# A fast down product's sum goes to the residual through ScalarE and an accumulating DMA

## The chip, the cores and the metric

The kernel runs on one core of a Trainium2 chip. A core has a matrix engine (TensorE, PE in the profile; its weight loads are the row PEld), three engines for elementwise work (VectorE, DVE; ScalarE, ACT; GpSimd, POOL), an engine that only issues DMAs here (SyncE, SP), and 16 DMA engines that all queues share. Engines run their own instruction streams in order and wait for each other on semaphores. Matmuls write to PSUM, a small memory that VectorE and ScalarE read; all else lies in SBUF.

The metric is device time in microseconds, lower is better: 2209.68 us before the change, the median of three runs (2209.25 to 2211.64).

## The reference

A two-layer encoder over 528 tokens (512 and 16 learned ones) of width 1024. A layer is FFN, mixer, FFN; the change touches the FFNs alone.

```python
def swiglu(x, w_gate, w_up, w_down):
    return (jax.nn.silu(x @ w_gate) * (x @ w_up)) @ w_down
...
    for l in range(DEPTH):
        h = h + 0.5 * swiglu(rmsnorm(h, norm_gains[l, 0]),
                             ffn_w_gate[l, 0], ffn_w_up[l, 0], ffn_w_down[l, 0])
        h = h + mixer(rmsnorm(h, norm_gains[l, 1]), ...)
        h = h + 0.5 * swiglu(rmsnorm(h, norm_gains[l, 2]),
                             ffn_w_gate[l, 1], ffn_w_up[l, 1], ffn_w_down[l, 1])
    return rmsnorm(h, final_norm)[:, N_META:]
```

All of it is float32. Width of the hidden layer: 2816, that is 22 chunks of 128, handled as 11 pairs.

## The kernel before

**Numbers.** Activations lie with channels on the 128 partitions and tokens along the row, in chunks of 128 channels; `hall` holds the residual `h`, eight chunks of 528 tokens. TensorE multiplies in a format with fewer bits, so each operand is split into a high part (`hi`, a rounding cast by ScalarE) and a low part (`lo`, the difference, by VectorE), and each product is three matmuls: hi by hi, hi by lo, lo by hi. Weights are split in the same way: ScalarE casts a block of 128 x 1024 (`whi`, L287), VectorE subtracts (`wlo`, L288). `W.make` runs that three to four blocks ahead of TensorE, `W.fetch` loads nine ahead on SP's queue.

**Seven products for eight.** The FFN's products are done by a fast scheme on 2 x 2 blocks (the block rows of the weights, and two halves of the tokens or the channels), with seven products named 1 to 7 where the plain way has eight. The sums of weight blocks that it needs are made partly by VectorE (L253, L256, L297) and partly by accumulating DMAs on GpSimd's queue (`W.add`, L208), each behind a plain load of the other summand. One product is 24 matmuls.

**The down projection.** The 11 pairs of hidden chunks are handled in groups of 4, 4 and 3 (`GROUPS`). The first two groups' down products use the seven-product scheme (`fast_down`, steps "S"): for each of two halves of the output chunks (`dq` 0 and 1), seven products accumulate in PSUM. Products 1, 6, 7 and 4 share one accumulator ("X"), 2 has its own ("Y"), 5 and 3 share one ("Z"). After each product the accumulator's running sum, 128 x 2 x 264 (for the last FFN 128 x 2 x 256), is added to two residual chunks' half (L719, L720), while accumulation goes on for the next product on top of it. So the next product on the same accumulator waits until the sum has been read. The third group is done in the plain way (`down`).

A block of such products, one for each of two groups in each of four FFNs, so eight blocks, is written out in `ffn_steps`: parts of products 1, 2 and 5 for `dq` 0 (three of the four hidden pairs, before the last pair is ready), then their rest, and then eleven products in the order that `AB` gives, `dq` in turn: 1 of dq 1, 6, 2 of dq 1, 7, 3, 4, and 6, 5, 7, 3, 4 of dq 1. Between the last five stand the first products of the next pair of the up projection (1, 2, 6, 5; L598).

The operands of the down products ("1", "2", "5", "6", "7", "3", "4") are made from the block's hidden values: differences by VectorE (`difference`, L678), the high part by ScalarE (L673, L670), the low part by VectorE (L674, L671). Operand "6" is made last of those that the block's start needs.

**What sets the order.** The tile framework's scheduler orders each engine's instructions within what the program's dependencies allow; pools of buffers set the waits. Touched pools: `t` (six tiles of 128 x 528), `wsa` and `wsb` (three each, sums of weights), `wraw` (three plain weight blocks), `whi` and `wlo` (four each), and the PSUM pairs (four). GpSimd's queue carries the weight sums' accumulating DMAs and nothing else. The residual is read again by the next block's adds, by the third group's adds (L564) and, after those, by the next norm.

Of the kernel before, what the change touches and what calls it, by code (L numbers as in the profile page):

```python
# [14 lines left out]
ALU = mybir.AluOpType  # L15
# [313 lines left out]
def build(tc, ctx, xt, wts, win, par, w2, const, umask, out):  # L329
    nc = tc.nc  # L330
    V, S, G, TE = nc.vector, nc.scalar, nc.gpsimd, nc.tensor
# [30 lines left out]
    def nm(p):  # L362
        count[0] += 1
        return f"{p}{count[0]}"
# [3 lines left out]
    def slot(tag, dtype=F32, n=None):  # L368
        return slots[tag].tile([P, T], dtype, tag=tag, name=nm(tag))[:, : n or live[0]]
# [11 lines left out]
    def pair(second=False):  # L381
        return (slots["s2"] if second else pss).tile([P, 2, 512], F32, tag="s2" if second else "ss", name=nm("ss"))
# [27 lines left out]
    def v2(ap):  # L410
        return ap.rearrange("p (a b) -> p a b", a=2)
# [161 lines left out]
    def ffn(l, f, norm, done, following):  # L573
# [112 lines left out]
        def operands_behind(g, dq, c):  # L686
            if (dq, c) == (1, "1"):
                difference(g, 1, 1, 3)
                operand(g, "7")
            elif (dq, c) == (1, "2"):  # L690
                operand(g, "3")
                difference(g, 2, 2, 0)
                operand(g, "4")

        def fast_down(g, dq, c, part):
            last = sum(GROUPS[: g + 1]) - 1
            kinds = ("ss", "s2") if last % 2 == 0 else ("s2", "ss")
            st = made.setdefault(("S", g, dq), {})
            where = {"2": "Y", "5": "Z", "3": "Z"}.get(c, "X")
            begin = c in "125"  # L700
            if part != 2:
                if begin:
                    st[where] = pair(kinds[{"Y": 0, "Z": 1, "X": dq}[where]] == "s2")
                st["w"] = st.get("w", {})
                st["w"][c] = W.op((l, f), NPAIR + QUADS * g + dq, c, ahead=AHEAD_MADE - 1)
            acc = st[where][:, :, :w]
            hi, lo = st["w"][c]
            xs = sets[g, c]
            for k in {1: range(3), 2: range(3, 4), 3: range(4)}[part]:
                for j in range(2):  # L710
                    for i, (a, b) in enumerate(((hi, 0), (hi, 1), (lo, 0))):
                        TE.matmul(acc[:, j], a[:, j, k], xs[b][:, k], start=bool(begin and k == 0 and i == 0),  # L712
                                  stop=k == 3 and i == 2, skip_group_check=not begin)
            if part == 1:
                return
            st["w"].pop(c)
            for m, q in {"1": [(0, 0)], "2": [(0, 0)], "5": [(1, 1)], "6": [(0, 1)], "3": [(0, 1)], "7": [(1, 1)],
                         "4": [(1, 0)]}[c]:
                to = hall[:, 4 * dq + m : 4 * dq + m + 3 : 2, q * w : (q + 1) * w]  # L719
                V.tensor_tensor(to, to, acc, ALU.add)  # L720
            if dq == 1:
                sets.pop((g, c))
            operands_behind(g, dq, c)
# [24 lines left out]
        for i, step in enumerate(steps):  # L748
            if step[0] == "P":
                if step[1:] == (0, "5") and norm.acc is None:  # L750
                    for c in range(KC):
                        norm.square(c)
                product_of_pair(*step[1:])
                if step[1:] == (0, "5"):
                    rs, up = norm.rs(True)
                    W.behind = prev_act[0]
                if step[1] in (2, 3) and step[2] in "6574":
                    m = next(risen)
                    V.scalar_tensor_tensor(h(m), h(m), -1.0, up, ALU.mult, ALU.mult)
                if i == last_op:  # L760
                    close_pools(norm.pools)
                    following()
            elif step[0] == "S":
                fast_down(*step[1:])
            elif step[0] == "O":
                g, last = step[1:]
                ks = slice(3, 4) if last else slice(0, 3)
                operands_of(g, ks, "215" if last else "125")
                difference(g, 0, 3, 0, ks)
                if last:  # L770
                    operand(g, "6")
            else:
                down(*step[1:])
# [597 lines left out]
```

## Time and profile before

| what | value |
|---|---|
| runs | 2209.68 us median, 2209.25 to 2211.64, n = 3 |
| profiled execution, its own time | 2211.05 us |
| its span, first to last instruction | 2209.2 us |
| granted TensorE clock | 0.997 |
| HBM read | 289.94 MB |

The profile is of one execution. Its page gives the busy time and share of each engine, the DMA queues, the chain of work that ended last (followed back from the last instruction, each step to what released it or to the instruction before it on its engine), and groups of instructions by source line. A row of instructions reads: line, engine, operation, destination tile <- source tiles, shapes. In a timeline a row begins with start and duration in us, and the bracket at its end is idle time of that engine before it and who ended it. In a table of waits a row is "who <- for whom: us in total, times, longest". In a table of windows a row is the stretch, its length, busy us and (instructions) of PE, PEld, DVE, ACT and POOL, the granted clock, the mean share of the 16 DMA engines that is busy, and GB/s. Matmuls are pipelined, so their durations overlap and add up to more than the time they take.

### The profile page before, as it was taken

How to read it: one execution, taken by the hardware profiler on the slowest of the kernel's cores; microseconds unless marked ns; L12 is line 12 of the kernel's file. 1: busy time of each engine (PE TensorE's matmuls, PEld its weight loads, DVE VectorE, ACT ScalarE, POOL GpSimd, SP SyncE). 2: the span in 40 equal slices, each digit the busy share in tenths (PEclk: the TensorE clock that was granted, in tenths of full speed). 3: DMA queues.
4: the chain of work that ended last, by engine and by line, in shares of the span. 5: the costliest groups of instructions: out<-in, count | busy, mean ns of one | idle time of the engine just before them, and what ended most of it. 6: DMA issues, size and time to landing. Idle time of an engine off the chain costs nothing.

```text
span 2209.2 us, 40079 instructions
## 1 busy us (share of the span) xinstructions
PE 2162.4 (98%) x16506; PEld 2070.2 (94%) x16506; DVE 1785.4 (81%) x2703; ACT 1214.1 (55%) x1779; POOL 101.8 (5%) x120
## 2 busy tenths in 40 slices
PE   7999999999999999999999999999999999999998
PEld 6999999989999999999999999999788888999997
DVE  7897978486886689889789979775879767997987
ACT  7544545344785555454575445453457836554543
POOL 1000000000000001000010000000000001000100
PEclk9999999999999999999999999999999999999999
DMA  9775753212113468666567757432121145776752
GB/s 268 189 204 160 191 152 106 82 49 68 49 39 122 114 167 205 190 182 187 162 163 186 207 164 191 143 110 77 49 84 51 42 133 152 198 202 181 189 165 67
DMA packets 87463, 311.41 MB, mean 141 GB/s; under 512 B 9712, under 2 KB 12144, under 8 KB 87280
## 3 DMA queue, kind: packets, MB, share of 16 engines
q1 hardware_dynamic: 68624, 245.53, 32.9%
q0 software_dynamic: 16704, 60.82, 15.8%
q8 instruction: 130, 2.13, 0.4%
q10 hardware_dynamic: 1952, 2.50, 0.4%
q14 instruction: 53, 0.43, 0.1%
HBM read 289.94 MB, written 2.10 MB: 132 GB/s over the span
## 4 chain that ended last, share of the span: by engine, by line
PE 81%; DVE 11%; ACT 4%; issue 2%; DMA 2%; SPq 0%; DVEq 0%; ACTq 0%
PE ss L598 37%; PE mm L465 13%; PE ss L712 11%; PE ss L465 10%; PE sm L465 2%; DVE wlo L288 2%; DMA w<-win 2%; PE sm L1074 1%; PE ss L1049 1%; DVE g L678 1%; ACT whi L287 1%; PE sm L1090 1%; DVE h L720 1%; PE ss L471 1%; PE sm L1091 1%
## 5 line engine op out<-in xcount | busy, mean ns | idle before, releaser
L598 PE MATMUL ss<-xc,whi 128*128 128x264 f32 (+1 forms) x4928 | 907.2, 285 | 15.5 <-ACT whi L287 7.4
L598 PEld LDWEIGHTS ss<-xc,whi 128*128 128x128 f32 x4928 | 767.2, 189 | 20.4 <-ACT c L602 8.4
L598 PE MATMUL ss<-xc,wlo 128*128 128x264 f32 (+1 forms) x2464 | 702.5, 285 | 8.8 <-DVE wlo L288 8.8
L598 PEld LDWEIGHTS ss<-xc,wlo 128*128 128x128 f32 x2464 | 466.5, 189 | 11.1 <-DVE wlo L288 10.9
L288 DVE TENSOR_TENSOR wlo<-w,whi 128x1024 fp32r<-128x1024 f32 (+1 forms) x337 | 408.1, 1217 | 63.4 <-ACT whi L287 63.2
L287 ACT CAST whi<-w 128x1024 fp32r<-128x1024 f32 (+1 forms) x337 | 350.0, 1050 | 163.3 <-PE ss L598 80.5
L465 PE MATMUL mm<-x,whi 128*128 128x264 f32 (+1 forms) x1712 | 384.6, 315 | 0.0
L465 PEld LDWEIGHTS mm<-x,whi 128*128 128x128 f32 x1712 | 278.3, 188 | 16.5 <-issue 1.0
L465 PE MATMUL mm<-x,wlo 128*128 128x264 f32 (+1 forms) x856 | 266.0, 315 | 0.0
L712 PE MATMUL ss<-g,whi 128*128 128x264 f32 (+1 forms) x1280 | 237.4, 284 | 0.0
L287 ACT CAST whi<-raw 128x1024 fp32r<-128x1024 f32 x126 | 132.3, 1050 | 163.4 <-PE mm L465 102.3
L602 ACT COPY c<-ss 128x528 f32<-128x528 f32 (+1 forms) x132 | 78.5, 594 | 258.6 <-PE ss L598 258.6
L288 DVE TENSOR_TENSOR wlo<-raw,whi 128x1024 fp32r<-128x1024 f32 x126 | 153.9, 1222 | 59.0 <-ACT whi L287 58.1
L712 PEld LDWEIGHTS ss<-g,whi 128*128 128x128 f32 x1280 | 198.4, 188 | 0.1
L712 PE MATMUL ss<-g,wlo 128*128 128x264 f32 (+1 forms) x640 | 181.3, 283 | 0.0
L465 PEld LDWEIGHTS mm<-x,wlo 128*128 128x128 f32 x856 | 159.6, 188 | 8.5 <-issue 0.7
L465 PE MATMUL ss<-g,whi 128*128 128x264 f32 (+2 forms) x900 | 166.3, 299 | 0.0
L465 PEld LDWEIGHTS ss<-g,whi 128*128 128x128 f32 x900 | 131.7, 188 | 5.3
L208 POOL DMA_DIRECT2D w<-win x60 | 52.7, 878 | 1574.7 <-DVE wlo L288 582.5
L712 PEld LDWEIGHTS ss<-g,wlo 128*128 128x128 f32 x640 | 120.5, 188 | 0.0
L444 ACT ACTIVATE c<-c 128x528 f32<-128x528 f32 (+1 forms) x88 | 56.6, 643 | 98.5 <-DVE c L642 98.4
L465 PE MATMUL ss<-g,wlo 128*128 128x264 f32 (+2 forms) x450 | 106.2, 300 | 0.0
(267 smaller groups left out, 3370.2 us busy)
## 6 DMA issues: line engine op xcount, KB each, us to landing
w<-win SPq DMA_DIRECT2D x335, 512.0 KB, 4.5
raw<-wts SPq DMA_DIRECT2D x126, 512.0 KB, 3.3
w<-win POOLq DMA_DIRECT2D x60, 512.0 KB, 7.4
s<-win POOLq DMA_DIRECT2D x24, 512.0 KB, 7.2
w<-s POOLq DMA_DIRECT2D x24, 512.0 KB, 5.6
s<-w POOLq DMA_DIRECT2D x8, 512.0 KB, 9.6
h<-xt SPq DMA_DIRECT2D x3, 528.0 KB, 6.8
out<-h ACTq DMA_DIRECT2D x4, 256.0 KB, 2.4
```

The source lines that it names most:

```text
L208: self.nc.gpsimd.dma_start(t, src, accum_op=ALU.add)
L287: nc.scalar.copy(hi[:, cs], w[:, cs])
L288: nc.vector.tensor_tensor(lo[:, cs], w[:, cs], hi[:, cs].bitcast(F32), ALU.subtract)
L444: prev_act[0] = S.activation(*args, **kw).ins
L465: TE.matmul(acc.half[i][:width], lhs, rhs[:, acc.spans[i]], start=first, stop=last)
L471: TE.matmul(a, weights, x[:, hs], start=True, stop=True)
L598: TE.matmul(acc[:, j], a[:, j, k], b[:, at], start=bool(begin and k == 0 and i == 0), stop=k == len(x) - 1 and i == 2, skip_group_check=no ...
L602: W.behind = S.copy(part(st, q), acc).ins
L678: V.tensor_tensor(r[into][:, ks], r[a][:, ks], r[b][:, ks], ALU.subtract)
L712: TE.matmul(acc[:, j], a[:, j, k], xs[b][:, k], start=bool(begin and k == 0 and i == 0), stop=k == 3 and i == 2, skip_group_check=not begin)
L720: V.tensor_tensor(to, to, acc, ALU.add)
L1049: TE.matmul(s[:n, i, :HF], lhs, kh[:, hs], start=True, stop=False)
```

## The change

After each fast down product, VectorE's add of the running sum to the residual goes. ScalarE copies the sum from PSUM to a `t` tile in SBUF, and GpSimd's queue issues a DMA that adds the tile to the residual, in SBUF.

```diff
@@ -717,7 +717,9 @@
             for m, q in {"1": [(0, 0)], "2": [(0, 0)], "5": [(1, 1)], "6": [(0, 1)], "3": [(0, 1)], "7": [(1, 1)],
                          "4": [(1, 0)]}[c]:
                 to = hall[:, 4 * dq + m : 4 * dq + m + 3 : 2, q * w : (q + 1) * w]
-                V.tensor_tensor(to, to, acc, ALU.add)
+                t = v2(slot("t"))
+                S.copy(t, acc)
+                G.dma_start(to, t, accum_op=ALU.add)
             if dq == 1:
                 sets.pop((g, c))
             operands_behind(g, dq, c)
```

`slot("t")` takes the next of the six `t` tiles; `v2` shows it as 2 x 264.

## The prediction

> **What bounds the kernel now.** I read the page first, then the waits of TensorE alone, then the chain and the timelines of one block of down products.
>
> ```profile
> span 2209.2 us, 40079 instructions
> PE 2162.4 (98%) x16506; PEld 2070.2 (94%) x16506; DVE 1785.4 (81%) x2703; ACT 1214.1 (55%) x1779; POOL 101.8 (5%) x120
> ...
> PE 81%; DVE 11%; ACT 4%; issue 2%; DMA 2%; SPq 0%; DVEq 0%; ACTq 0%
> PE ss L598 37%; PE mm L465 13%; PE ss L712 11%; PE ss L465 10%; PE sm L465 2%; DVE wlo L288 2%; DMA w<-win 2%; PE sm L1074 1%; PE ss L1049 1%; DVE g L678 1%; ACT whi L287 1%; PE sm L1090 1%; DVE h L720 1%; PE ss L471 1%; PE sm L1091 1%
> ```
>
> TensorE sets the end; VectorE is full enough to hold it up in places, ScalarE is half empty, GpSimd's queue almost idle. The edited add (L720) has 1% of the chain. What TensorE really loses beside the edited code stands in its own waits:
>
> ```profile
> PE ss L712 <- DVE c L674: 3.4, 8, 0.6
> ```
>
> Eight waits, one for each block of down products (four FFNs, two fast groups each), 3.4 us together. The first block runs from 106 to 166 us. Its chain:
>
> ```profile
> 121.00 0.61 DVE h L720
> ...
> 123.09 1.23 DVE h L720 x2
> 124.32 1.24 DVE c L674
> 125.56 0.04 issue
> 125.60 11.92 PE ss L712 x96
> ```
>
> From 121 to 125.6 us the chain runs through VectorE: it finishes the low half of operand "6" (L674, ending at 125.55) after three residual adds. Then come 96 matmuls without a gap, 11.92/96 = 0.124 us each. TensorE's own rows show the price:
>
> ```profile
> 120.75 0.69 PE L712 MATMUL ss<-c,whi 128*128 128x264 f32 x2
> ...
> 124.80 0.41 PE L712 MATMUL ss<-g,whi 128*128 128x264 f32 x2
> 125.60 0.39 PE L712 MATMUL ss<-c,whi 128*128 128x264 f32 x1 [0.40 <-DVE c L674]
> ```
>
> At pace the third row would start at 124.80 + 2 x 0.124 = 125.05; it starts 0.55 us later. The pair at 120.75 takes 0.69 instead of 0.41, a gap of 0.28 before operand "5", which is finished ahead of the first residual add and so isn't helped. Behind 125.60 the block has no hole.
>
> **Part 1: the adds leave VectorE.** 112 instructions go, 14 a block:
>
> ```profile
> L720 DVE TENSOR_TENSOR h<-h,ss x112: 680/697/705, 120.9 to 2115.2; 128x528 f32<-128x528 f32 x84, 128x512 f32<-128x512 f32 x28
> ```
>
> That is 112 x 0.697 = 78 us of VectorE, but it is worth only what TensorE waits for. I re-time VectorE's queue by the order in which the changed kernel is built (an order, no times) and these durations:
>
> ```profile
> 120.57 0.43 DVE L674 TENSOR_TENSOR c<-g,c 128x264 fp32r<-128x264 f32 x1
> 120.91 0.70 DVE L720 TENSOR_TENSOR h<-h,ss 128x528 f32<-128x528 f32 x1
> 121.53 1.22 DVE L288 TENSOR_TENSOR wlo<-w,whi 128x1024 fp32r<-128x1024 f32 x1
> 122.66 0.43 DVE L678 TENSOR_TENSOR g<-g,g 128x264 f32<-128x264 f32 x1
> 123.00 1.31 DVE L720 TENSOR_TENSOR h<-h,ss 128x528 f32<-128x528 f32 x2
> 124.29 1.26 DVE L674 TENSOR_TENSOR c<-g,c 128x1056 fp32r<-128x1056 f32 x1
> ```
>
> New order: the L674 of 120.57, then the small difference (L678) at once, 121.00 to 121.43; one wlo to 122.6; the large difference for operand "4", which the builder has moved up into the place of the adds, 1.25 us, to 123.7; then the L674 of operand "6", 123.65 to 124.9. Of the 2.0 us that three adds free, 1.2 go to the moved difference. "6" is ready 0.65 us earlier, 0.15 us before TensorE's pace needs it (125.05). The gap closes: 0.55 x 8 = 4.4 us, and a little more in the last FFN; I take **-4.5**. Bounds: 0 if VectorE gets nothing done sooner, -6.7 if the 0.28 closes too ((0.55 + 0.28) x 8).
>
> **Part 2: 112 copies on ScalarE.** Nearest row, the same shape from PSUM:
>
> ```profile
> L602 ACT COPY c<-ss x132: 566/599/605, 24.2 to 2160.5; 128x528 f32<-128x528 f32 x99, 128x512 f32<-128x512 f32 x33
> ```
>
> 112 x 0.6 = 67 us, 8.4 a block. ScalarE is in order, and behind the waiting copy stand the weight casts and operand casts. Around the gap it now does:
>
> ```profile
> 120.10 2.00 ACT L287 CAST whi<-w 128x1024 fp32r<-128x1024 f32 x2 [0.29 <-PE ss L712]
> 122.00 1.05 ACT L287 CAST whi<-s 128x1024 fp32r<-128x1024 f32 x1
> 123.18 1.08 ACT L673 CAST c<-g 128x1056 fp32r<-128x1056 f32 x1
> 124.76 1.07 ACT L673 CAST g<-g 128x1056 fp32r<-128x1056 f32 x1 [0.50 <-PE ss L712]
> ```
>
> In the new order one weight cast (to 121.1) is followed by the copy of sum "1" (to 121.6), the high half of "6" (waits for the difference at 121.43; to 122.7, in time for VectorE at 123.65), the copies of "2" and "5" (to 123.8), then the two other weight casts (to 125.8 instead of 123.05). The earlier of these feeds the product after "6", due at 125.6 + 24 x 0.124 = 128.5; its low half is made by 126.1, 2.4 us to spare. The cast of operand "7" moves from 124.76 to about 126.3; it is due one product later. The copies release PSUM no later than the adds did: the accumulator that "6" writes is free at 121.6. Six t tiles serve the fourteen copies of a block, so the seventh copy (about 135) waits for the landing of the first DMA (issued about 121.7), which even the slowest row of part 3 puts before 130. Cost taken: 0. If the 2.4 us were gone, each us of delay would cost 1 us a block, 8 in all.
>
> **Part 3: 112 accumulating DMAs.** Each moves 128 x 2 rows of 1056 B. Prices:
>
> ```profile
> q1 hardware_dynamic: 68624, 245.53, 32.9%
> q0 software_dynamic: 16704, 60.82, 15.8%
> ...
> q10 hardware_dynamic: 1952, 2.50, 0.4%
> ```
>
> GpSimd's queue (q0, all of it accumulating) takes 0.158 x 2209.2 x 16/16704 = 334 ns a packet of 3.64 KB on average; by bytes a row of 1056 B costs 97 ns, so one add is 256 x 97/16 = 1.55 us of all 16 engines. Plain packets: 169 ns for 3.58 KB on q1, 72 ns for 1.28 KB on q10, so small ones cost 1.2 times as much a byte: 1.85 us. Ends: 1.55, and 5.3 if a row costs as much as a whole packet. I take 1.6, since q10 falls so nearly with size. A block gets 22 us (75 at the far end). The room for it:
>
> ```profile
> 118.00:143.00 25.00, 24.58 (x200) 24.16 (x199) 24.73 (x29) 14.13 (x15) 0.63 (x1) 1.00 0.56 151
> 143.00:168.00 25.00, 25.00 (x207) 25.00 (x207) 20.54 (x22) 9.31 (x10) 1.73 (x2) 1.00 0.83 252
> 166.00:231.00 65.00, 65.00 (x534) 64.87 (x532) 51.08 (x63) 32.91 (x41) 4.39 (x5) 1.00 0.61 166
> 106.00:231.00 125.00, 124.08 (x1012) 123.31 (x1010) 107.31 (x127) 63.64 (x75) 8.72 (x10) 1.00 0.67 186
> ```
>
> The last column but one is the DMA share. From one block to the next 0.33 x 125 = 41 us are free, against 22. The first seven adds (11 us) fit the 0.44 x 25 = 11 free in 118 to 143; the other seven meet 4 free us in 143 to 168, and some 7 us of work spill into the next stretch, where 0.39 is free. Does that delay a weight load that matters?
>
> ```profile
> w<-win SPq DMA_DIRECT2D x335, 512.0 KB, 4.5
> raw<-wts SPq DMA_DIRECT2D x126, 512.0 KB, 3.3
> w<-win POOLq DMA_DIRECT2D x60, 512.0 KB, 7.4
> ```
>
> Loads that run among accumulating DMAs (the first row) land 1.2 us later than those that hardly do (the second). The tightest weight is the one summed by GpSimd here:
>
> ```profile
> 144.62 0.86 POOL L208 DMA_DIRECT2D w<-win  x1 [26.00 <-DVE h L720]
> ```
> ```profile
> 151.75 1.06 ACT L287 CAST whi<-w 128x1024 fp32r<-128x1024 f32 x1 [1.86 <-PE ss L598]
> ```
> ```profile
> 160.58 2.94 PE ss L598 x24
> ```
>
> Issued at 144.62, cast at 151.75 (a cast that waits for TensorE, not for the DMA), used at 160.58: 160.58 - 151.75 - 1.06 - 1.22 = 6.5 us to spare. In GpSimd's in-order queue it now stands behind the seventh of the block's adds, whose sum is copied at about 135.5, 9 us before 144.62; the later adds queue behind it. Nothing reads the residual again until the next block or the last group. Each issue takes GpSimd 0.86 us, and it has time. Cost taken: 0; at the far end 75 - 41 = 34 us a block.
>
> [...]
>
> **Sum.** The profiled execution took 2211.05 us, 1.85 more than its span and 1.37 more than the median; 2211.05 - 4.5 + 0 + 0 = 2206.55, which against the median of 2209.68 is **2205.2**, -0.20%.
>
> **The rivals.**
> *Nothing moves*: 0.15 us of margin for operand "6" is thin, and its high half now waits behind a copy. If "6" comes when it did, 2209.7 (+-2).
> *The whole chain goes*: the chain counts 0.61 + 1.23 = 1.84 us of adds a block, 14.7 in all, which would give 2195. TensorE's rows allow 0.83 a block: 2203.0.
> *ScalarE becomes the gate* (slower): in order, it holds weight casts behind copies that wait for TensorE. It decides once the 2.4 us above are used up; at 1 us beyond, 2209.7 + 8 = 2218. For it: three copies stand ahead of that cast. Against: VectorE's adds of 123.00 show no wait, so both sums were complete about when ScalarE will reach them (122.7), and ScalarE is 55% busy.
> *DMA full* (slower): small accumulating rows cost a fixed time rather than a byte price. It decides at 41/14 = 2.9 us an add, 183 ns a row. At 334 ns a block loses 34 us: 2209.7 + 272 = 2482; just past the point, some 10 us. [...] Against: 41 free us.
>
> **How the numbers follow.** Gap closes 0.45 (own range 2203.5 to 2207; 0.33 of it beyond 0.2%); whole chain 0.09; nothing moves 0.24; ScalarE 0.10; DMA full 0.12. Taking 0.2% (4.4 us, about what a measurement of this kernel can tell from no change): faster 0.33 + 0.09 = 0.42, same 0.12 + 0.24 = 0.36, slower 0.22. The forecast sits on that line, so faster and same are near each other. Range: low 2202.5, just past the most that the rows allow; high 2222, which takes in the ScalarE case and the mild DMA case, with 0.13 left above.
>
> **What would show it.** Right: the eight waits of L712 on L674 fall from 3.4 us to under 1; VectorE's busy time falls by 78 us, ScalarE's rises by 67; q0 gains 30 MB and some 170 us of share (8%); no new waits of casts on DMA. Wrong: L598 or L712 waiting for wlo or whi in the blocks (ScalarE or DMA, told apart by what the casts wait for), q0's share up by over 15%, or the L674 wait unchanged.

## The result, and the profile after

The changed kernel takes 2348.48 us (median, 2342.14 to 2356.71, n = 6) against 2210.98 us (2209.25 to 2215.65, n = 6) for the kernel before in the same series: 1.0626 times as long, 95% interval 1.0609 to 1.0642. It is slower by 138 us, where 4.5 us less were forecast. The profiled execution took 2355.6 us.

The page of the changed kernel, the lines that answer to those shown of before (span, busy times, the chain by engine, GpSimd's DMA queue as packets, MB and share of 16 engines, two DMA issues with their us to landing):

```profile
span 2353.7 us, 40352 instructions
PE 2207.6 (94%) x16506; PEld 2106.0 (89%) x16506; DVE 1714.7 (73%) x2591; ACT 1263.9 (54%) x1891; POOL 237.9 (10%) x232
...
q0 software_dynamic: 47168, 90.88, 22.9%
...
PE 57%; DVE 13%; DMA 11%; issue 10%; ACT 6%; POOL 2%; SPq 0%; POOLq 0%; DVEq 0%; ACTq 0%
...
w<-win SPq DMA_DIRECT2D x335, 512.0 KB, 4.7
...
h<-t POOLq DMA_DIRECT2D x84, 264.0 KB, 5.6
```

The span grew by 144.5 us. TensorE's busy time grew by 2207.6 - 2162.4 = 45.2 us with the same 16506 matmuls, so they ran slower somewhere; the other 99.3 us is TensorE standing still. TensorE's share of the chain fell from 81% to 57%, and what came in is mostly DMA (2% to 11%) and "issue" (2% to 10%), not ScalarE (4% to 6%).

The 99.3 us are found in the waits. Of the changed kernel:

```profile
ACT whi L287 <- DMA w<-win: 198.6, 20, 16.0
POOL h L722 <- issue: 196.4, 48, 8.2
...
PE ss L598 <- ACT whi L287: 84.7, 17, 8.9
...
ACT t L721 <- DMA h<-t: 48.0, 20, 5.0
...
PE ss L598 <- DVE wlo L288: 28.3, 31, 3.5
...
PE ss L712 <- DVE c L674: 1.4, 5, 0.4
```

and of the kernel before:

```profile
PE ss L598 <- DVE wlo L288: 8.8, 8, 3.1
...
ACT whi L287 <- DMA w<-win: 7.6, 5, 2.3
...
PE ss L598 <- ACT whi L287: 7.4, 1, 7.4
```

TensorE waits for the two halves of split weights (L598, the next pair's up projection): 84.7 + 28.3 us instead of 7.4 + 8.8, 96.8 more. It waits for a cast, and the cast waits for a DMA that brings `w`: 198.6 us instead of 7.6, in only 20 places. The loads on SP's queue land in 4.7 us (4.5 before), so it isn't they. The second line names the place: the new adds on GpSimd (L722) stand 196.4 us "at issue", with nothing the profile shows to wait for. (All of GpSimd's idle time before them is 483.0 us by the page; much of the rest is put down to ScalarE's casts, on which no add depends.) The wait that the change could remove did shrink (last line, 3.4 to 1.4).

GpSimd's timeline over the first block of the changed kernel (start, us; the bracket is GpSimd's idle time before):

```profile
123.00 1.21 POOL L722 DMA_DIRECT2D h<-t  x1 [4.94 <-ACT t L721]
129.43 1.22 POOL L722 DMA_DIRECT2D h<-t  x1 [5.22 <-ACT g L670]
135.97 1.20 POOL L722 DMA_DIRECT2D h<-t  x1 [5.32 <-issue]
...
159.44 1.20 POOL L722 DMA_DIRECT2D h<-t  x1 [6.47 <-issue]
160.16 1.44 POOL L208 DMA_DIRECT2D w<-win  x1
163.59 1.21 POOL L722 DMA_DIRECT2D h<-t  x1 [1.99 <-issue]
...
188.05 1.44 POOL L208 DMA_DIRECT2D w<-win  x1
```

The seven adds go out 4.6 to 7.7 us apart (left out are 141.05, 145.70 and 151.76), though ScalarE has copied three sums by 123.2. An add waits for its copy and for some earlier DMAs of its queue; L670 in a bracket is just what ended at about that time. By the DMA records the first six land at 129.1, 135.6, 140.7, 145.4, 151.4 and 159.1: each next add starts 0.3 to 0.4 us after the one before has landed. One add is in flight at a time. Only at 145.70 does the program itself wait for the add just before (in the whole trace 54.0 us, 15 times); the others have nothing left to wait for. The weight sum (L208) that went out at 144.62 before stands behind seven of them and goes out at 160.16; the next, at 157.64 before, goes out at 188.05. But note that the weight sum goes out only 0.72 us after the add ahead of it, without waiting for it to land, and that the add behind it waits again.

What this does downstream, in ScalarE's and TensorE's timelines of the changed kernel:

```profile
167.17 1.04 ACT L287 CAST whi<-w 128x1024 fp32r<-128x1024 f32 x1 [15.05 <-DMA w<-win]
```
```profile
159.12 0.28 PE L712 MATMUL ss<-g,wlo 128*128 128x264 f32 x1
168.27 0.81 PE L598 MATMUL ss<-xc,whi 128*128 128x264 f32 x2 [8.87 <-ACT whi L287]
...
169.91 0.64 PE L598 MATMUL ss<-xc,whi 128*128 128x264 f32 x2
...
170.57 0.64 PE L598 MATMUL ss<-xc,whi 128*128 128x264 f32 x2
...
172.55 0.41 PE L598 MATMUL ss<-xc,whi 128*128 128x264 f32 x2
...
172.92 0.40 PE L598 MATMUL ss<-xc,whi 128*128 128x264 f32 x2
```

The cast comes at 167.17, where it came at 151.75, and TensorE stands from 159.4 to 168.3. The 6.5 us to spare were real; the sum was 15.5 us late. After the pause three matmuls take 0.66 us (169.91 to 170.57) until 172.5, then 0.37. The windows of the same kernel (length, busy us of PE, PEld, DVE, ACT and POOL, granted clock, DMA share, GB/s) show why:

```profile
159.10:168.30 9.20, 0.33 (x4) 0.12 (x2) 0.05 (x1) 1.13 (x2) 3.37 (x3) 0.67 0.73 116
168.30:172.50 4.20, 3.75 (x15) 3.44 (x16) 4.17 (x4) 4.20 (x6) 1.21 (x1) 0.50 0.41 95
172.50:190.00 17.50, 17.50 (x146) 17.50 (x145) 12.57 (x13) 5.76 (x8) 4.55 (x4) 1.00 0.76 184
```

The granted clock falls to one half during the pause and stays there for 4.2 us after it. (Finer windows of the same trace have the clock at 1.00 from 161.0 to 162.0, 0.65 from 162.0 to 163.0 and 0.50 from there on: it falls at about 162.3, 2.9 us after TensorE has stopped, and 4.2 us of work pass before it is back.) This is most of the second item, the 45.2 us of slower matmuls: by the trace's clock records TensorE is busy for 87.5 us at half the clock, 6.7 before, and half of the difference is 40 us. The same pattern stands in all eight blocks, with a pause of 4.9 to 8.9 us in each and further ones behind it.

**The theory, called RING in the experiments.** The DMAs that are in flight on GpSimd's queue share a room of fixed size, which the program sets (`dynamic_dma_scratch_size=1024`, L1364, in bytes), and a DMA's part of it is given back when it lands. What a DMA takes of it is counted by q0's packets: (47168 - 16704)/112 = 272 for one add, 17 for each of 16 engines; the weight sums have 16704/116 = 144, or 9. (The expectations call these descriptors; no trace shows what the room holds.) In the timeline 17 + 9 fit (the weight sum of 160.16 goes out before the add of 159.44 lands at 163.27), and 17 + 17 don't: in the whole trace no two adds are in flight together. That leaves a room of 26 to 33 at 1024 B. RING takes 32, that is 32 bytes for each; this value was the author's assumption, and no trace shows it.

Against it stand FULL (the engines are full, or the small rows cost a fixed time), SHAPE (it is the form of the add, two rows a partition, and not its count) and SCALAR (the copies hold ScalarE up). FULL is weak already: 0.229 x 2353.7 x 16 - 0.158 x 2209.2 x 16 = 3039 us for 30464 packets, 100 ns a packet.

### The profile page after: what moved, and what is told of

It is laid out like the page before. It is cut to its first block, busy times and chain, and to the rows that moved or that the text cites. A ratio compares the mean times of both kernels' runs of the same rounds, so it can differ in the third digit from the quotient of the medians.

```text
span 2353.7 us, 40352 instructions
## 1 busy us (share of the span) xinstructions
PE 2207.6 (94%) x16506; PEld 2106.0 (89%) x16506; DVE 1714.7 (73%) x2591; ACT 1263.9 (54%) x1891; POOL 237.9 (10%) x232
## 3 DMA queue, kind: packets, MB, share of 16 engines
q0 software_dynamic: 47168, 90.88, 22.9%
## 4 chain that ended last, share of the span: by engine, by line
PE 57%; DVE 13%; DMA 11%; issue 10%; ACT 6%; POOL 2%; SPq 0%; POOLq 0%; DVEq 0%; ACTq 0%
PE ss L598 24%; PE mm L465 12%; DMA w<-win 9%; PE ss L465 9%; DVE wlo L288 4%; PE ss L712 4%; POOL h L722 2%; PE sm L465 2%; ACT whi L287 2%; DMA h<-t 1%; PE sm L1076 1%; PE ss L1051 1%; PE ss L471 1%; PE sm L1092 1%; ACT t L444 1%
## 5 line engine op out<-in xcount | busy, mean ns | idle before, releaser
L598 PE MATMUL ss<-xc,whi 128*128 128x264 f32 (+1 forms) x4928 | 939.9, 292 | 93.2 <-ACT whi L287 84.7
L598 PEld LDWEIGHTS ss<-xc,whi 128*128 128x128 f32 x4928 | 793.4, 196 | 101.2 <-ACT whi L287 88.2
L598 PE MATMUL ss<-xc,wlo 128*128 128x264 f32 (+1 forms) x2464 | 719.6, 292 | 28.3 <-DVE wlo L288 28.3
L288 DVE TENSOR_TENSOR wlo<-w,whi 128x1024 fp32r<-128x1024 f32 (+1 forms) x337 | 406.4, 1217 | 199.0 <-ACT whi L287 198.6
L598 PEld LDWEIGHTS ss<-xc,wlo 128*128 128x128 f32 x2464 | 481.3, 195 | 36.8 <-DVE wlo L288 36.8
L287 ACT CAST whi<-w 128x1024 fp32r<-128x1024 f32 (+1 forms) x337 | 348.4, 1048 | 295.1 <-DMA w<-win 198.6
L465 PEld LDWEIGHTS mm<-x,whi 128*128 128x128 f32 x1712 | 278.4, 188 | 16.6 <-issue 1.0
L712 PE MATMUL ss<-g,whi 128*128 128x264 f32 (+1 forms) x1280 | 237.8, 285 | 2.4 <-ACT g L673 1.2
L712 PEld LDWEIGHTS ss<-g,whi 128*128 128x128 f32 x1280 | 198.9, 189 | 3.9 <-ACT g L673 1.6
L722 POOL DMA_DIRECT2D h<-t x112 | 135.1, 1206 | 483.0 <-issue 196.4
L712 PE MATMUL ss<-g,wlo 128*128 128x264 f32 (+1 forms) x640 | 181.8, 284 | 1.5 <-DVE wlo L288 1.5
L208 POOL DMA_DIRECT2D w<-win x60 | 65.2, 1086 | 1092.7 <-DMA w<-win 434.1
L288 DVE TENSOR_TENSOR wlo<-s,whi 128x1024 fp32r<-128x1024 f32 x84 | 102.4, 1220 | 60.6 <-ACT whi L287 60.5
L712 PEld LDWEIGHTS ss<-g,wlo 128*128 128x128 f32 x640 | 120.7, 189 | 1.9 <-DVE wlo L288 1.9
```

What stands on the lines that cost most here:

```text
L208: self.nc.gpsimd.dma_start(t, src, accum_op=ALU.add)
L287: nc.scalar.copy(hi[:, cs], w[:, cs])
L288: nc.vector.tensor_tensor(lo[:, cs], w[:, cs], hi[:, cs].bitcast(F32), ALU.subtract)
L465: TE.matmul(acc.half[i][:width], lhs, rhs[:, acc.spans[i]], start=first, stop=last)
L598: TE.matmul(acc[:, j], a[:, j, k], b[:, at], start=bool(begin and k == 0 and i == 0), stop=k == len(x) - 1 and i == 2, skip_group_check=no ...
L722: G.dma_start(to, t, accum_op=ALU.add)
```

## The experiments

Eight kernels. The first four ran beside 25 runs of the kernel before (median 2211.52 us), the other four beside 13 (2210.20 us); each ratio is to those.

### More room

```diff
-    nc = bacc.Bacc(..., dynamic_dma_scratch_size=1024)
+    nc = bacc.Bacc(..., dynamic_dma_scratch_size=2752)
```

> [...] Theory RING: in the changed kernel each residual add is issued only when the one before it has landed (issues at 129.4, 136.0, 141.1, 145.7, 151.8, 159.4 us, each 0.3 us after a landing), because two adds' descriptors (2 x 17 an engine) don't fit where one and a weight block's (17 + 9) do; the weight sums stand behind them. With 2.7 times the space four or five adds fit: issues follow the copies, the weight casts wait for no DMA, time 2200 to 2215. Rival FULL: the DMA engines have no room for 112 adds of small rows; then it stays at 2320 or more. Rival SHAPE: GpSimd finishes a two-row add before it issues another, whatever the space: stays at 2340 to 2355.

Measured: 2213.76 us (2207.24 to 2220.06, n = 10), ratio 1.0010 (0.9998 to 1.0023). GpSimd's timeline of this run:

```profile
129.63 3.65 POOL L722 DMA_DIRECT2D h<-t  x3 [4.81 <-DMA h<-t]
...
142.13 1.95 POOL L208 DMA_DIRECT2D w<-win  x1
...
161.55 1.19 POOL L722 DMA_DIRECT2D h<-t  x1 [10.81 <-DMA h<-t]
162.27 1.43 POOL L208 DMA_DIRECT2D w<-win  x1
```

and its waits:

```profile
POOL h L722 <- DMA h<-t: 129.2, 21, 13.2
...
ACT whi L287 <- DMA w<-win: 18.2, 9, 7.7
...
POOL h L722 <- issue: 1.5, 3, 0.9
```

One number, and 135 of the 138 us are gone: the wait at issue falls from 196.4 to 1.5 us (all idle time before the adds from 483.0 to 240.1), three adds go out in a row, the first weight sum at 142. So neither FULL nor SCALAR caused the loss, since the same adds and copies are all still there. But the gain isn't there either. What is left are waits between the adds themselves (129.2 us: a later add waits for an earlier one to land), which still hold the second weight sum to 162.27 instead of 157.64. So the casts still wait 18.2 us for DMAs (7.6 before), where none was expected. The adds land in 8.6 us, the loads on SP's queue in 5.2 instead of 4.5.

### The kernel before with the same room

The same line in the kernel before, as a control.

> The kernel before, with 2752 bytes as in e1: a control. RING: its 116 weight sums take 9 descriptors an engine and are seldom more than two in flight, so no change: 2206 to 2213. If it gains more than 5 us, then e1 has to be compared with this kernel and not with the one before.

Measured: 2210.37 us (2208.75 to 2211.76, n = 10), ratio 0.9994 (0.9984 to 1.0004). The room alone gives nothing; its sums, 9 packets an engine and at most three in flight in the trace of before, didn't lack it.

### ScalarE's copy without the DMA

```diff
                 t = v2(slot("t"))
                 S.copy(t, acc)
-                G.dma_start(to, t, accum_op=ALU.add)
+                V.tensor_tensor(to, to, t, ALU.add)
```

> ScalarE's copy stays, the accumulating DMA goes: VectorE adds the t tile to the residual. RING, FULL and SHAPE (the DMA is the cost): 2205 to 2218, near the kernel before. Rival SCALAR (the copy in ScalarE's in-order queue is the cost): 2300 or more.

Measured: 2209.25 us (2206.73 to 2211.19, n = 10), ratio 0.9991 (0.9982 to 1.0000). All 112 copies are there and cost nothing: SCALAR falls. The gap before operand "6" closes too. Only one such wait is left in this kernel (0.4 us, against eight with 3.4 us), though three waits of L712 for other operands, 2.3 us together, have come in:

```profile
PE ss L712 <- DVE c L674: 0.4, 1, 0.4
```

VectorE's timeline of this run, in a block that starts 0.4 us earlier than before:

```profile
122.13 0.70 DVE L722 TENSOR_TENSOR h<-h,t 128x528 f32<-128x528 f32 x1
122.75 1.25 DVE L674 TENSOR_TENSOR c<-g,c 128x1056 fp32r<-128x1056 f32 x1
123.92 1.32 DVE L722 TENSOR_TENSOR h<-h,t 128x528 f32<-128x528 f32 x2
```

All adds are still VectorE's, but one instead of three stands ahead of operand "6" (L674); the other two go behind it. So it was less VectorE's load that made the gap than the place of these adds in its order.

### Each add as two DMAs

```diff
-                G.dma_start(to, t, accum_op=ALU.add)
+                for u in range(2):
+                    G.dma_start(to[:, u], t[:, u], accum_op=ALU.add)
```

Twice the DMAs, each with one row a partition, and by this run's q0 (48960 - 16704)/224 = 144 packets, 9 an engine; the room stays at 1024 B.

> Each residual add is issued as two DMAs, one for each of the two chunks (128 rows of 1056 B, 9 descriptors an engine each); bytes and rows are the same. RING: three such halves fit together instead of one whole add, so about one and a half adds are in flight: the wait mostly goes, 2205 to 2270. FULL: same rows, 2340 or more. SHAPE (one row a partition isn't held up): 2200 to 2220.

Measured: 2236.65 us (2233.02 to 2238.81, n = 4), ratio 1.0112 (1.0095 to 1.0129). The waits:

```profile
POOL h L723 <- issue: 159.4, 82, 6.4
...
ACT whi L287 <- DMA w<-win: 86.4, 18, 12.6
```

In units of 9, three fit where one of 17 did: three halves go out within 2.64 us (from 144.12), while one takes 5.3 us to land (median), so 1.5 adds are in flight instead of one. Four fifths of the loss go, with the same bytes and rows: against FULL. That 159.4 us at issue remain, and 25 us of time, speaks against SHAPE, which expected the whole loss to go.

### How much room is needed

The last doubt is whether it is the count that decides. With RING's assumed 32 bytes, 1088 B is 34 x 32: exactly two adds, if the count is right.

```diff
-    nc = bacc.Bacc(..., dynamic_dma_scratch_size=1024)
+    nc = bacc.Bacc(..., dynamic_dma_scratch_size=1088)
```

> The changed kernel with a descriptor space of 1088 B in place of 1024. RING counts an add as 17 descriptors per DMA engine and the space as 32 at 1024 B, so 34 at 1088 B: exactly two adds. If a full space can be used, two adds now run at a time, the 196 us that GpSimd's adds wait at issue fall below 100, and the time falls from 2348 to 2220-2290. If one place must stay empty, or if it is not the count but a wait of the program (a semaphore, an earlier add of the same residual half) that holds the adds, nothing changes: 2340-2360. The 1152 B run tells the last two apart.

> The changed kernel with 1152 B: 36 places, so two adds (34) with two left over. RING: two adds at a time whatever the rule for the last place, 2220-2290 us, the wait at issue below 100 us. A wait of the program would leave 2340-2360. A cost that grows smoothly with the space would give a fourteenth of the way from 2348 to 2214 (128 of 1728 B more): about 2338.

Measured at 1088 B: 2221.83 us (2218.82 and 2224.83), ratio 1.0050 (1.0032 to 1.0069); at 1152 B: 2225.11 us (2222.56 and 2227.65), ratio 1.0065 (1.0047 to 1.0083). At 1088 B:

```profile
128.53 1.20 POOL L722 DMA_DIRECT2D h<-t  x1 [3.90 <-ACT g L673]
131.39 1.20 POOL L722 DMA_DIRECT2D h<-t  x1 [1.66 <-DMA h<-t]
...
148.92 0.92 POOL L208 DMA_DIRECT2D w<-win  x1 [0.17 <-issue]
```
```profile
POOL h L722 <- issue: 81.5, 29, 4.8
```

64 bytes more bring 126 of the 138 us back. An add follows another after 2.9 us, while one takes 6.3 us to land (median of the page), so two are in flight, and the weight sum goes out at 148.9 instead of 160.2. Another 64 bytes do nothing more; by RING's count 36 places hold no third add. A step where it was predicted and flat ground behind it: that the room decides is shown.

The exact count isn't. By the issues and landings in the traces, the first add of a block, with two weight sums still in flight (17 + 9 + 9 = 35), is held at 1024 B until one of them has landed (123.00, 0.3 us after a landing at 122.68). At 1088 B it goes out with both in flight, in all eight blocks (the first at 123.43, after sums of 117.55 and 118.89), though 34 places wouldn't hold it. Nothing larger goes out at 1088 or 1152 B; two adds and a sum (43) are held. So, counted in this way, the runs show a room of 27 to 33 at 1024 B and of 35 to 42 at 1088 and 1152 B, and the assumed 32 bytes a place isn't quite right. What the right count is, no run shows.

### Three adds by DMA, eleven on VectorE

The room stays at 1024 B. Only the three adds ahead of operand "6" take the new way.

```diff
                 to = hall[:, 4 * dq + m : 4 * dq + m + 3 : 2, q * w : (q + 1) * w]
+                if dq == 1 or c not in "125":
+                    V.tensor_tensor(to, to, acc, ALU.add)
+                    continue
                 t = v2(slot("t"))
```

> Descriptor space 1024 B as before; only the first three adds of each block (products 1, 2 and 5 of dq 0, those ahead of operand 6) go by copy and accumulating DMA, the other eleven stay on VectorE. RING: the three go out one after the other at about 123, 129 and 135 and are down by 141, before the weight sum that goes out at 144.6; no cast waits for it, and the gap before operand 6 closes: 2203-2209 us, the waits of L712 on L674 below 1 us. If it is the traffic or the path of the adds themselves that costs, three fourteenths of the loss stay: 138 x 3/14 = 30, about 2240.

Measured: 2205.63 us (2203.33 to 2208.21, n = 9), ratio 0.9976 (0.9966 to 0.9986), 4.6 us less than before and the best of all. GpSimd's timeline of this run (its block starts 3.7 us later than in the changed kernel):

```profile
127.64 1.21 POOL L725 DMA_DIRECT2D h<-t  x1 [5.60 <-ACT t L724]
134.15 1.22 POOL L725 DMA_DIRECT2D h<-t  x1 [5.30 <-issue]
138.48 1.20 POOL L725 DMA_DIRECT2D h<-t  x1 [3.12 <-issue]
145.51 0.94 POOL L208 DMA_DIRECT2D w<-win  x1 [5.83 <-DMA w<-win]
159.53 0.87 POOL L208 DMA_DIRECT2D w<-win  x1 [13.08 <-DVE h L721]
```
```profile
ACT whi L287 <- DMA w<-win: 7.0, 5, 2.1
```

The three adds are held one behind the other here as well (5.30 and 3.12 us at issue), but there is nothing behind them that is in a hurry. The two weight sums go out 0.9 and 1.9 us after they did before, in a block that itself starts 3.3 us later. The casts wait 7.0 us for DMAs (7.6 before), and TensorE's list of waits has no L712 any more. The serial issue costs nothing by itself; it costs what waits behind it.

### Eleven adds by DMA, three on VectorE

The reverse condition (`dq == 0 and c in "125"` stays on VectorE).

> The reverse: the first three adds of a block on VectorE, the other eleven by copy and accumulating DMA, descriptor space 1024 B. RING: four adds instead of seven stand ahead of the first weight sum, at about 128.6, 134, 140 and 145, so it goes out near 146 instead of 160 and its cast no longer waits; the second weight sum still stands behind five more adds, near 174 against 158 before, and is 5 to 10 us late. So about half of the loss: 2250-2300 us, with the 3.4 us of L712 on L674 back. If every add costs alike: 138 x 11/14 = 108, about 2320.

Measured: 2250.58 us (2245.72 and 2255.45), ratio 1.0180 (1.0157 to 1.0204), at the low end of RING's range, far under the 2320 of a loss shared by all adds.

```profile
148.44 1.45 POOL L208 DMA_DIRECT2D w<-win  x1
...
174.21 1.43 POOL L208 DMA_DIRECT2D w<-win  x1
```
```profile
PE ss L712 <- DVE c L674: 4.2, 11, 0.5
```

The first weight sum is late by 3.8 us (148.44 for 144.62), within its 6.5 us to spare; the second is late by 16.6 (174.21 for 157.64; 5 to 10 were expected), beyond it. The gap before operand "6" is back (last line). So three adds of fourteen, taken away from the front, save 97 of the 138 us, where an equal share would be 30.

## Why the prediction was wrong, point by point

**Part 1, the adds leave VectorE: right.** Operand "6" was forecast for 123.65 to 124.9 us. VectorE's timeline of the changed kernel:

```profile
123.21 1.25 DVE L674 TENSOR_TENSOR c<-g,c 128x1056 fp32r<-128x1056 f32 x1
```

It ends at 124.46 (125.55 before), in a block that begins 0.4 us earlier, so the rival "nothing moves" is refuted. The waits of L712 for L674 fell to 1.4 us in five places, not quite to under 1. The term of -4.5 us agrees with what is left when nothing else is in its way: -4.6 us with three adds by DMA (0.14 to 0.34% by the interval). That the closed gap alone gives it isn't shown, since the copies without the DMA close it nearly as well and gain 2.3 us. "The whole chain goes" (2203.0) isn't reached.

**Part 2, 112 copies at no cost: right.** A copy takes 0.596 us (0.6 from the nearest row), and the run that keeps the copies and leaves out the DMAs is not slower than before. ScalarE did not become the gate. That the seventh copy must wait for the first DMA's landing "before 130" was right too (129.1). The tiles ran out later, because one add at a time returns a tile only every 4.6 to 7.7 us: 48.0 us of waits of the copies for landings, of which 6.6 remain with 2752 B. Whether these waits, which hold the casts behind them, cost TensorE anything beside the late weight sums, no run separates.

**Part 3, the price of the rows: right; their place in the queue: wrong.** Taken were 97 ns a row and 1.6 us an add. Measured: 100 ns a packet by q0's share, so 272 x 100/16 = 1.7 us. q0's share rose by 7.1%, where 8% were forecast. The rival "DMA full" had its limit at 183 ns and is refuted.

The step that failed is this one: "In GpSimd's in-order queue it now stands behind the seventh of the block's adds, whose sum is copied at about 135.5, 9 us before 144.62; ... Each issue takes GpSimd 0.86 us, and it has time. Cost taken: 0". It took for granted that an add goes out when its sum is ready. The order was right, and so were the 6.5 us that the weight had to spare. But an add doesn't hold GpSimd for 0.86 us, nor for the measured 1.20: it holds the queue until the one before it has landed, and the next goes out 4.6 to 7.7 us after it. Seven of them from 123.00 reach to 159.44, not 135.5, and the weight sum is 15.5 us late. The trace of before couldn't show it: its GpSimd queue carried 116 DMAs of 144 packets, at most three in flight at a time, and none that failed to fit. What could be read before the run was 16704/116 = 144 packets, the declared 1024 bytes, and that the adds have twice the rows; that it was a resource that could run out was not asked.

**The sum and the range.** The cost taken as 0 was worth 99 us of pauses and 45 us of slower matmuls, some 40 of them by the halved clock, in the profiled execution. The prediction had said that an L598 which waits for `whi` would show it wrong, and that what the casts wait for would tell why. They wait for DMAs, though the engines had room: a transfer that starts late, not one that takes long. None of the four rivals was this one, and the range ended 126 us below.

**Open.** With 2752 B the changed kernel doesn't reach the one with three adds by DMA (2.2 us above the kernel before in its series, against 4.6 below). Its waits between adds, the slower landings and the later second weight sum are candidates; its single profile shows little more waiting of TensorE, and its runs spread over 13 us. No run separates them.

## What to carry to other kernels

A queue that issues in order is priced by when each entry may start, not by how long an issue takes: ask what each entry must find free (a tile, an earlier landing, room in what the program declares), and what stands behind it. When work moves to a queue, count the packets of one transfer against the room the program declares; a transfer of 128 partitions with two rows each had 272 packets here, a plain one 144, and 64 bytes of room were worth 126 us. And look for the few instructions that make the wait: of the fourteen adds of a block, the three ahead of the wait brought the gain, and what the others added was loss.

## What the runs showed of the hardware that was not expected

- With `dynamic_dma_scratch_size` at 1024 B the adds on GpSimd's queue were held at issue for 196.4 us, at 1088 B for 81.5, at 1152 B for 96.9, at 2752 B for 1.5. The profile has no releaser for such a wait (it says "issue", or names what ended by chance).
- An add's accumulating packets take 100 ns each (987 B on average), where those of 3.64 KB take 334: the price goes nearly by bytes.
- An issue of such an add holds GpSimd for 1.20 us, a plain sum for 0.87.
- A pause of TensorE of 8.9 us (159.4 to 168.3) was followed by 4.2 us at half the granted clock. With pauses of 99 us in all came 45 us more of busy time, some 40 of it at half the clock.
